# Decode's small copies made by ScalarE alone: placing the probabilities and spreading the queries in a hybrid decoder step

## The chip, the cores and the metric

The kernel runs on one core of one Trainium2 chip. The metric is the device time of one execution in microseconds (us), as a median over runs. The engines are TensorE (PE; its weight loads are PEld), VectorE (DVE), ScalarE (ACT), GpSimd (POOL) and SyncE (SP), which issues most DMAs. Each engine works through its own list of instructions in order and waits on semaphores for the others.

## What is computed

One layer of a hybrid decoder serves 512 prompt tokens and 32 sample tokens (8 sequences of 4) with shared weights, in float32. It is a feed-forward net, a mixer and a second feed-forward net, each with norms around it. The mixer has a gated linear recurrence (HGRN2) and latent softmax attention (MLA). The sample tokens also attend to 4096 past tokens each, whose latent rows (256 wide) and rotary keys (64 wide) lie in pages:

```python
def swiglu(x, wg, wu, wd):
    return (jax.nn.silu(x @ wg) * (x @ wu)) @ wd

# mla_attend, one block of queries
s = (jnp.einsum('bqhr,bsr->bhqs', ql, c_kv) + jnp.einsum('bqhd,bsd->bhqs', qr, k_rope)).astype(jnp.float32) * scale
s = jnp.where(k_pos[None, None, None, :] <= qp[None, None, :, None], s, -jnp.inf)
p = jax.nn.softmax(s, axis=-1).astype(c_kv.dtype)
return jnp.einsum('bhqs,bsr->bqhr', p, c_kv)

# layer
h = h + 0.5 * rmsnorm(swiglu(rmsnorm(h, norm_g[0]), wg[0], wu[0], wd[0]), norm_g[1])
m, c_kv, k_r, s_fin = mixer(rmsnorm(h, norm_g[2]), pos, past_ckv, past_kr, past_pos, s0, lb, ...)
h = h + rmsnorm(m, norm_g[3])
h = h + 0.5 * rmsnorm(swiglu(rmsnorm(h, norm_g[4]), wg[1], wu[1], wd[1]), norm_g[5])
```

## The kernel before

The tokens are split in two column parts, 0 and 1. The stages follow each other: the first feed-forward net, the mixer, then the second net for part 0 with the attention of the sample tokens to the past (decode) woven into it, then the output projection and the second net for part 1. Each product of two float32 matrices is made of three matmuls over a high and a low half of the operands. So each weight tile is loaded as `wraw`, ACT makes its high half `wh` by a cast (line 250), and DVE makes the low half `wl` as the difference (line 251). In the second net a gate product goes to DVE (`sil`, line 334), then through three ACT steps of a sigmoid (`sit`, lines 320 to 322), back to DVE (336), is multiplied by the up product (365) and split by ACT and DVE (170 and 171) into the operand of the down product (lines 259 and 288).

Decode handles each sample sequence in two halves of 2048 past tokens, 16 halves in all (class `Half`). A half goes through these steps:
- `gather`, `gather_r` (lines 1366, 1373): POOL issues indirect DMAs that bring latent rows and rotary keys into one of seven slots.
- `turn` (1381): DVE transposes pieces of these rows in 32 by 32 blocks into `kh`, ten for a half, two columns at a time.
- `score` (1393): PE multiplies the spread queries `qbd` by `kh` into two banks `s`; the results are copied to SBUF, one bank by ACT and one by DVE (1399), and DVE takes the row maximum (1401).
- `peak`: PE spreads the maximum (1405), DVE reduces it (1407) and makes the bias (1410), ACT takes the exponential (1411), DVE transposes it in blocks to `pt` (1413), and 16 copies place its blocks in `pbuf` (1417), in which each query's columns stand at its own place among zeros. Of each four copies, the one with g = 0 is made by DVE and the other three by ACT.
- `value` (1426): PE multiplies `pbuf` by the latent rows in two groups of eight products, c = 0 and c = 1; each reads the blocks of two of the four c of the copies. The sum is copied out by ACT (1429) and gathered by a small product (1434).

`qsplit` (1252) spreads the queries of one sequence: four copies out of `qrep`, which `decode_prep` has made (1243, 1245), into the operand `qbd` of the score products, each block at its own columns among zeros. Those of even g are made by DVE and those of odd g by ACT. It runs once for each of 8 sequences, and `qbd` has two buffers.

`decode()` is a generator that runs the steps of five halves at a time, each half some rounds behind the one before it; a round has five steps, `peak` is at its second step and `value` at its last. The loop at the end of the stage takes one step of decode and then as many steps of the net (`gb`) as keep the two in proportion (100 of the net's). This fixes the program's order. The order on each engine, and the slots of tiles, are then chosen by a planner with a timing model of its own, which follows the program's order as a priority; `tc.issue_after` adds an order by hand (the last `turn` of a round stands behind the maximum).

Of the kernel before, what the change touches and what calls it, by code (L numbers as in the profile page):

```python
# [110 lines left out]
def hybrid_step_kernel(  # L111
# [5 lines left out]
    nc = tc.nc  # L117
# [12 lines left out]
    def mk(shape, dt, tag, bufs=1, pool=None):  # L130
        return (pool or cur[-1]).tile(shape, dt, name=tag, tag=tag, bufs=bufs)
# [10 lines left out]
    def ps(name, tag="ps", own=False):  # L142
        if tag == "ps" and not own:
            tag = CYC[turns[0] % 4]
            turns[0] += 1
        return pp.tile([P, 512], F32, name=name, tag=tag, bufs=NPS[tag])
# [642 lines left out]
    with scope("mix") as mx_:  # L789
# [293 lines left out]
        with scope("at2"):  # L1083
# [163 lines left out]
            def qsplit(b):  # L1247
                q = qbd[b % 2]
                bs = slice(b * 16, b * 16 + 16)
                for g in range(4):  # L1250
                    gs = slice(g * 32, g * 32 + 32)
                    (nc.scalar.copy if g % 2 else nc.vector.tensor_copy)(q[gs, :, g % 2 * 16 : g % 2 * 16 + 16], qrep[gs, :, bs])

            def to_ffn(x):
                u4[x], part = parted_u(4, x)
# [7 lines left out]
            for i, (hd, x) in enumerate(heads):  # L1263
                if i + LOOK < len(heads):
                    if i + LOOK < NH:
                        prep(i + LOOK)
                    else:
                        qsplit_n(i + LOOK - NH, 1, qnb[:, i + LOOK - NH])
                    pe_.append(soft(*heads[i + LOOK]))
                if i < NH:  # L1270
                    latent(i)
                if i == PJ0:
                    pj = project(0, to_ffn)
                    next(pj)
                value(hd, x, pe_[i])
                if i == NH - 1:
                    dq = mk([P, 2, KQ * HS[1]], F32, "q1", pool=dK)
                    qbd = [dq[:, 0, k * 320 : (k + 1) * 320].rearrange("p (j q) -> p j q", j=10) for k in range(2)]
                    qrep = dq[:, 1, : 10 * P].rearrange("p (j q) -> p j q", j=10)
                    nc.gpsimd.memset(dq[:, 0, :640], 0.0)  # L1280
                if i == DP:
                    decode_prep()
                    qsplit(0)
                for _ in range(PJ[i]):
                    next(pj, None)
                if i in W1:
                    w0.append(weight([wcols((w_g, w_u)[W1.index(i)][1], 0, KD, 0)], KD))
# [14 lines left out]
    with scope("dec"):  # L1302
# [49 lines left out]
        class Half:  # L1352
# [31 lines left out]
            def score(self, st):  # L1384
                q = qbd[self.b % 2]
                if st == 0:
                    self.s = [ps("s", own=True) for _ in range(2)]
                for jj, j in enumerate(JS[st]):
                    for c in range(4):
                        for r in range(2):  # L1390
                            rs = slice(r * 64, r * 64 + 64)
                            kh = self.kh[st][rs, c // 2, c % 2 * 4 : c % 2 * 4 + 4, jj]
                            nc.tensor.matmul(self.s[r][c * 32 : c * 32 + 32, :P], q[rs, j], kh, start=st + jj == 0, stop=st == len(JS) - 1 and jj == 1, skip_group_check=True)  # L1393
                if st == 1 and self.i and self.b + 1 < NB:
                    qsplit(self.b + 1)
                if st < len(JS) - 1:
                    return
                for r in range(2):
                    (nc.vector.tensor_copy if r else nc.scalar.copy)(self.e[:, r * P : r * P + P], self.s[r][:, :P])
                self.mx = mk([P, 1], F32, "mxh", 2)  # L1400
                self.top = nc.vector.tensor_reduce(self.mx, self.e, axis=AX.X, op=ALU.max)

            def peak(self):
                pm = ps("pm", "pm")[:, :P]
                nc.tensor.matmul(pm, self.mx.broadcast_to([P, P]), ident, start=True, stop=True, skip_group_check=True)
                m = m3[:, self.i, self.bs]
                nc.vector.tensor_reduce(m, pm.rearrange("p (g q) -> p q g", q=16), axis=AX.X, op=ALU.max)
                mq = mk([P, 16], F32, "mq", 2)
                mb = mk([P, 1], F32, "mbd", 2)
                nc.vector.scalar_tensor_tensor(mq, m, -SCALE, selL, op0=ALU.mult, op1=ALU.mult, accum_out=mb)  # L1410
                nc.scalar.activation(self.e, self.e, AF.Exp, scale=SCALE, bias=mb, accum_out=Lc[:, self.i, 0, self.b : self.b + 1])
                pt = mk([P, ROWS, 32], F32, "pt", 2)
                nc.vector.transpose(pt.rearrange("p a k -> p (a k)"), self.e)  # L1413
                for c in range(4):
                    for g in range(4):
                        src = pt[c * 32 : c * 32 + 32, g // 2 * 4 : g // 2 * 4 + 4, g % 2 * 16 : g % 2 * 16 + 16]
                        (nc.scalar.copy if g else nc.vector.tensor_copy)(self.p[g * 32 : g * 32 + 32, c // 2, c % 2 * 4 : c % 2 * 4 + 4, self.i * 16 : self.i * 16 + 16], src)  # L1417

            def value(self, mate, c):
                i = self.i  # L1420
# [289 lines left out]
```

## Time and profile before

| | |
|---|---|
| median of 3 runs | 1250.35 us (1250.27 to 1250.57) |
| the profiled execution, own time | 1243.16 us |
| its span in the trace | 1241.4 us, granted clock 0.999 |
| decode's copies to `pbuf` (L1417) | 192 on ACT, 64 on DVE |
| spread of the queries (L1252) | 16 on ACT, 16 on DVE |

A profile is of one execution. Engines are listed with their busy time; "wl<-wraw,wh" is an instruction that writes the tile wl from wraw and wh, and L251 is a line of the kernel. Rows of a timeline give the start in us from the span's start, the length in us, the engine, line and operation, the shapes, how many were merged, and in brackets the engine's idle time before it and who ended it. The waits are listed as "who <- for whom: us in total, times, longest". The chain of waits goes back from the last instruction to what released it, or to the instruction before it on its engine. The decode stage is the stretch from 691 to 953 us.

### The profile page before, as it was taken

What the parts mean: (1) busy time and instruction counts of PE and PEld (TensorE: products, weight loads), DVE (VectorE), ACT (ScalarE), POOL (GpSimd) and SP (SyncE); (2) the same over time, 40 slices, a digit from 0 to 9 for tenths busy, and PEclk for the clock granted to TensorE, in tenths of its full rate; (3) what the DMA queues carried; (4) which work ended last, traced back from release to release, by engine and by line L of the source; (5) the groups of instructions that cost most, each with busy time, mean ns of one, the idle gap of its engine ahead of it and who ended that gap; (6) DMA issues with size and microseconds to landing.
All of it is one profiled execution on the core that took longest, in us unless ns stands there. A gap on an engine that the chain in (4) does not pass through costs nothing.

```text
span 1241.4 us, 29997 instructions
## 1 busy us (share of the span) xinstructions
PE 1215.0 (98%) x12366; PEld 1151.3 (93%) x12366; DVE 982.7 (79%) x1976; ACT 738.8 (60%) x1559; POOL 76.5 (6%) x80
## 2 busy tenths in 40 slices
PE   8999999999999999999999999999999999999997
PEld 6999999999999989988898888888888999999997
DVE  7897788878678888786877899999998778566665
ACT  7675545455366744545758766666656776554455
POOL 0000000000000000000001312322310000000000
PEclk9999999999999999999999999999999999999999
DMA  6232333232264213333233868878776635545451
GB/s 238 86 115 90 103 103 102 86 99 91 62 221 147 82 54 105 88 94 130 85 105 117 339 214 303 310 282 323 258 275 232 198 106 188 184 137 188 150 151 60
DMA packets 73113, 195.59 MB, mean 158 GB/s; under 512 B 12336, under 2 KB 27728, under 8 KB 68240
## 3 DMA queue, kind: packets, MB, share of 16 engines
q1 hardware_dynamic: 64512, 150.47, 37.3%
q0 software_dynamic: 7168, 41.95, 9.2%
q8 instruction: 97, 1.59, 0.5%
q10 hardware_dynamic: 1296, 1.26, 0.3%
q14 instruction: 40, 0.33, 0.1%
HBM read 183.97 MB, written 9.67 MB: 156 GB/s over the span
## 4 chain that ended last, share of the span: by engine, by line
PE 79%; DVE 11%; ACT 7%; issue 2%; DMA 2%; SPq 0%; DVEq 0%; ACTq 0%
PE acc L259 29%; PE acc L277 13%; PE dn L259 8%; PE Y L575 7%; PE X L575 4%; PE Z L575 4%; DVE kh L1381 3%; PE acc L731 3%; DVE wl L251 2%; ACT wh L250 1%; PE s L1393 1%; ACT pbuf L1417 1%; DMA wraw<-w_g 1%; PE pa L952 1%; PE o L1426 1%
## 5 line engine op out<-in xcount | busy, mean ns | idle before, releaser
L250 ACT CAST wh<-wraw 128x1024 fp32r<-128x1024 f32 (+2 forms) x194 | 185.0, 957 | 164.3 <-PE acc L259 103.7
L251 DVE TENSOR_TENSOR wl<-wraw,wh 128x1024 fp32r<-128x1024 f32 (+2 forms) x194 | 214.6, 1108 | 72.2 <-ACT wh L250 71.6
L277 PE MATMUL acc<-uha,wh 128*128 128x256 f32 (+1 forms) x528 | 155.5, 295 | 0.1
L277 PE MATMUL acc<-uha,wl 128*128 128x256 f32 (+1 forms) x528 | 150.0, 285 | 0.8 <-DVE wl L251 0.7
L277 PE MATMUL acc<-ula,wh 128*128 128x256 f32 (+1 forms) x528 | 150.5, 286 | 0.0
L259 PE MATMUL acc<-uhb,wh 128*128 128x288 f32 (+1 forms) x432 | 128.0, 296 | 0.0
L259 PE MATMUL acc<-uhb,wl 128*128 128x288 f32 (+1 forms) x432 | 127.0, 295 | 1.0 <-DVE wl L251 0.8
L259 PE MATMUL acc<-ulb,wh 128*128 128x288 f32 (+1 forms) x432 | 127.5, 295 | 0.0
L277 PEld LDWEIGHTS acc<-uha,wh 128*128 128x128 f32 x528 | 99.2, 188 | 8.8 <-issue 7.9
L277 PEld LDWEIGHTS acc<-uha,wl 128*128 128x128 f32 x528 | 99.2, 188 | 2.3 <-DVE wl L251 1.6
L277 PEld LDWEIGHTS acc<-ula,wh 128*128 128x128 f32 x528 | 99.4, 188 | 1.6 <-issue 1.2
L259 PEld LDWEIGHTS acc<-uhb,wl 128*128 128x128 f32 x432 | 81.2, 188 | 1.6 <-DVE wl L251 1.6
L259 PEld LDWEIGHTS acc<-uhb,wh 128*128 128x128 f32 x432 | 81.0, 187 | 0.2 <-ACT uhb L170 0.2
L259 PEld LDWEIGHTS acc<-ulb,wh 128*128 128x128 f32 x432 | 81.1, 188 | 0.1
L259 PE MATMUL dn<-hh,dh 128*128 128x272 f32 x256 | 74.3, 290 | 0.0
L259 PE MATMUL dn<-hh,dl 128*128 128x272 f32 x256 | 73.7, 288 | 0.0
L259 PE MATMUL dn<-hl,dh 128*128 128x272 f32 x256 | 73.6, 288 | 0.0
L277 PE MATMUL acc<-uhb,wh 128*128 128x272 f32 x176 | 52.8, 300 | 0.0
L1417 ACT COPY pbuf<-pt 32x64 f32<-32x64 f32 x192 | 46.5, 242 | 10.1 <-DVE pt L1413 7.3
L259 PE MATMUL acc<-hlb,wh 128*128 128x288 f32 x176 | 52.1, 298 | 0.0
L259 PE MATMUL acc<-hhb,wh 128*128 128x288 f32 x176 | 51.8, 298 | 0.0
L1393 PE MATMUL s<-kh,q 64*32 64x128 f32 x2560 | 48.0, 273 | 3.5 <-DVE kh L1381 3.5
(632 smaller groups left out, 3881.3 us busy)
## 6 DMA issues: line engine op xcount, KB each, us to landing
wraw<-w_u SPq DMA_DIRECT2D x66, 512.0 KB, 4.3
wraw<-w_g SPq DMA_DIRECT2D x65, 512.0 KB, 3.9
wraw<-w_d SPq DMA_DIRECT2D x40, 384.0 KB, 3.5
wraw<-w_in SPq DMA_DIRECT2D x24, 512.0 KB, 3.5
wraw<-w_d SPq DMA_DIRECT2D x32, 320.0 KB, 3.1
wraw<-w_d SPq DMA_DIRECT2D x16, 512.0 KB, 3.8
wraw<-w_o SPq DMA_DIRECT2D x16, 512.0 KB, 3.7
g_S<-state SPq DMA_DIRECT2D x4, 512.0 KB, 4.4
```

The source lines that it names most:

```text
L250: nc.scalar.copy(wh[:, :kt], w[:, :kt])
L251: nc.vector.tensor_tensor(wl[:, :kt], w[:, :kt], f32(wh[:, :kt]), op=ALU.subtract)
L259: nc.tensor.matmul(out, a, b, start=n == 0, stop=n == last)
L277: nc.tensor.matmul(acc[:, :n], a[:, k], b[:, k], start=k + i == 0, stop=k == kt - 1 and i == 2)
L575: nc.tensor.matmul(bank, a[p][:, k], b[q][:, k], start=first and k + n == 0, stop=k == 3 and n == 2, skip_group_check=True)
L731: nc.tensor.matmul(accs[x, d], wts[d][p][:, k], hs[k // 2][q][:, k % 2, x], start=k + n == 0, stop=k == nf - 1 and n == 2)
L952: nc.tensor.matmul(po[es, c].rearrange("p (n m) -> p n m", m=m), kx[:, cs], up(qx[:, cs], m), start=True, stop=True, skip_group_check=True)
L1381: nc.vector.transpose(kh[:, g].rearrange("p a j k -> p a (j k)"), src)
L1393: nc.tensor.matmul(self.s[r][c * 32 : c * 32 + 32, :P], q[rs, j], kh, start=st + jj == 0, stop=st == len(JS) - 1 and jj == 1, skip_group_c ...
L1417: (nc.scalar.copy if g else nc.vector.tensor_copy)(self.p[g * 32 : g * 32 + 32, c // 2, c % 2 * 4 : c % 2 * 4 + 4, self.i * 16 : self.i * ...
L1426: nc.tensor.matmul(o[g : g + 32, :R], self.p[:, c, a], self.craw[c][:, a], start=i + c == 0 and a < 4, stop=i + c == 2 and a >= 4, skip_gr ...
```

## The change

All 16 copies of `peak` and all 4 copies of `qsplit` are made by ScalarE. Per half, 4 of the 16 copies of 32 x 64 elements go from DVE to ACT, 64 in all; per sequence, 2 of the 4 copies of 32 x 160 elements, 16 in all. The copies read and write what they did before, and their place in the program's order stays. No other line differs.

```diff
             def qsplit(b):
...
-                    (nc.scalar.copy if g % 2 else nc.vector.tensor_copy)(q[gs, :, g % 2 * 16 : g % 2 * 16 + 16], qrep[gs, :, bs])
+                    nc.scalar.copy(q[gs, :, g % 2 * 16 : g % 2 * 16 + 16], qrep[gs, :, bs])
...
             def peak(self):
...
-                        (nc.scalar.copy if g else nc.vector.tensor_copy)(self.p[g * 32 : g * 32 + 32, c // 2, c % 2 * 4 : c % 2 * 4 + 4, self.i * 16 : self.i * 16 + 16], src)
+                        nc.scalar.copy(self.p[g * 32 : g * 32 + 32, c // 2, c % 2 * 4 : c % 2 * 4 + 4, self.i * 16 : self.i * 16 + 16], src)
```

## The prediction

> **What bounds the kernel now.** I read the page's engine shares first, then the busy time of each engine by stretches of the decode stage, then what waits for what there, then the chain of waits, and last the order of instructions on ScalarE (ACT) and VectorE (DVE) around the copies that move.
>
> ```profile
> PE 1215.0 (98%) x12366; PEld 1151.3 (93%) x12366; DVE 982.7 (79%) x1976; ACT 738.8 (60%) x1559; POOL 76.5 (6%) x80
> ```
>
> Over the whole span TensorE (PE) is the full engine. All copies that move start between 666 and 951 us, so only that stage counts. Cut where its regimes change (columns: stretch, its length, then busy us and instructions of PE, PEld, DVE, ACT, POOL, the clock, DMA):
>
> ```profile
> 753.00:797.60 44.60, 44.43 (x806) 39.48 (x806) 40.45 (x85) 28.95 (x78) 13.28 (x12) 1.00 0.89 317
> 797.60:839.00 41.40, 39.98 (x818) 34.30 (x818) 39.27 (x90) 26.82 (x76) 12.81 (x12) 1.00 0.77 270
> 884.40:943.00 58.60, 58.16 (x1105) 50.25 (x1103) 54.41 (x122) 34.74 (x95) 11.91 (x11) 1.00 0.70 243
> sum 262.00, PE 255.78 PEld 224.28 DVE 244.06 ACT 166.56 POOL 65.31; mean PE 42.63 PEld 37.38 DVE 40.68 ACT 27.76 POOL 10.89
> ```
>
> The sum runs from 691 to 953 us. PE idles 262.00 - 255.78 = 6.2 us in it: no help to any other engine can gain more than about that. DVE is nearly as full (39.27 of 41.40), ACT is not (26.82). In 753 to 797.6 PE is the bound; in 797.6 to 839 it idles 1.4 us, and there the question is whether DVE or ACT is late.
>
> ```profile
> DVE wl L251 <- ACT wh L250: 16.8, 21, 2.9
> PEld s L1393 <- DVE kh L1381: 5.4, 7, 1.7
> PE s L1393 <- DVE kh L1381: 3.5, 7, 1.4
> PEld o L1426 <- ACT pbuf L1417: 1.9, 5, 0.6
> ```
>
> DVE, though full, itself waits 16.8 us for ACT's casts (wh); PE waits for DVE's transposes (kh), and in five places for ACT's pbuf copies. So the two engines hand a chain to and fro. The chain of waits says how much of it is the copies:
>
> ```profile
> by line: DVE kh L1381 25.9%; ACT pbuf L1417 12.5%; DVE wl L251 11.6%; issue 7.4%; ACT wh L250 6.8%; PE s L1393 4.2%; ACT sit L321 3.6%; DVE hla L171 3.1%; DVE sil L336 3.0%; ACT sit L322 3.0%; DVE sil L365 2.5%; ACT sit L320 2.2%; DVE mxh L
> 808.84 0.24 ACT pbuf L1417
> ...
> 950.65 0.24 ACT pbuf L1417
> ...
> 735.86 0.14 DVE pbuf L1417
> ...
> 937.44 0.04 DVE pbuf L1417
> ...
> 742.71 0.15 DVE q L1252
> ...
> 891.55 0.24 DVE q L1252
> ```
>
> The first line is of 797 to 840 us. Below it stand the first and the last piece of each kind: 72 pieces of ACT's pbuf copies, which are all 12 of a half in 6 of the 16 halves; 16 pieces of DVE's, in 4 halves; 8 pieces of DVE's spread of the queries, 1.4 us together. The copies that lie on the chain are ACT's more than DVE's. That decides my forecast: the change lengthens the link that is late more often.
>
> **The change part by part.** Prices first (minimum/median/maximum ns):
>
> ```profile
> L1417 ACT COPY pbuf<-pt x192: 239/242/247, 735.5 to 950.6; 32x64 f32<-32x64 f32 x192
> L1417 DVE COPY pbuf<-pt x64: 140/183/188, 735.9 to 948.4; 32x64 f32<-32x64 f32 x64
> L1252 DVE COPY q<-q x16: 223/234/257, 666.1 to 891.6; 32x160 f32<-32x160 f32 x16
> L1252 ACT COPY q<-q x16: 320/324/327, 666.8 to 887.3; 32x160 f32<-32x160 f32 x16
> ```
>
> [...]
>
> In a row the copies run at this pace, and this stands around them (times of start, length):
>
> ```profile
> 808.84 3.07 ACT L1417 COPY pbuf<-pt 32x64 f32<-32x64 f32 x12 [1.16 <-DVE pt L1413]
> 811.93 1.05 ACT L250 CAST wh<-wraw 128x1024 fp32r<-128x1024 f32 x1
> 813.86 0.42 ACT L322 ACTIVATE sit<-sit 128x256 f32<-128x256 f32 x1
> ...
> 809.32 0.74 DVE L1417 COPY pbuf<-pt 32x64 f32<-32x64 f32 x4
> 813.00 1.23 DVE L251 TENSOR_TENSOR wl<-wraw,wh 128x1024 fp32r<-128x1024 f32 x1 [0.73 <-ACT wh L250]
> 814.31 0.43 DVE L336 TENSOR_TENSOR sil<-sil,sit 128x256 f32<-128x256 f32 x1
> ```
>
> A half's 12 copies take 3.07 us on ACT, 0.256 each; 16 will take 4.1, that is 1.02 more. DVE loses its four, 0.75 us. Behind the copies on ACT stand the cast of the next weight (wh, 0.02 us after the last copy) and the three steps of the gate's sigmoid (sit); DVE waits for the cast already (0.73 us idle) and then for sit. Freeing DVE's 0.75 us here only makes that idle time longer: the next link moves by the full 1.02 us.
>
> So I cost the old chain anew with the order of instructions kept. It is a lower bound of the stage's new length, since the links stay dependent and another path can only be longer.
> - Probabilities on ACT: 6 halves by 4 copies by 0.256 = +6.1 us.
> - Probabilities on DVE: 4 halves by 0.75 = -3.0 us.
> - Spread on DVE: -1.4 us.
> - Spread on ACT: two spreads run together at 666 us, six later ones alone. The later ones lie ahead of an idle time of ACT, shortest at 742 and next at 828, against 0.67 us for two copies more:
>
> ```profile
> 743.05 0.84 ACT L250 CAST wh<-wraw 128x768 fp32r<-128x768 f32 x1 [0.29 <-PE acc L277]
> ...
> 747.61 0.92 DVE L251 TENSOR_TENSOR wl<-wraw,wh 128x768 fp32r<-128x768 f32 x1
> ...
> 827.69 0.67 ACT L1252 COPY q<-q 32x160 f32<-32x160 f32 x2
> 829.13 0.84 ACT L250 CAST wh<-wraw 128x768 fp32r<-128x768 f32 x1 [0.77 <-PE acc L277]
> ...
> 666.83 1.00 ACT L1252 COPY q<-q 32x160 f32<-32x160 f32 x3
> 667.85 1.05 ACT L250 CAST wh<-wraw 128x1024 fp32r<-128x1024 f32 x1
> ```
>
> At 742 only 0.29 of 0.67 is covered by ACT's wait, but DVE's share of that weight comes 3.7 us after the cast, behind transposes, so it hides the rest; I take nothing for the six. If their cover were gone they would cost 6 by 0.67 = 4.0 us. The two at 666.83 have a cast right behind three of their copies: three more by 0.333, +1.0 us.
>
> Together +6.1 - 3.0 - 1.4 + 1.0 = +2.7 us.
>
> What is late next: the value matmuls, which read pbuf. In the two halves where DVE's copies hold up kh and PE stalls most, ACT's own copies end just ahead of value's second group:
>
> ```profile
> 836.79 3.06 ACT L1417 COPY pbuf<-pt 32x64 f32<-32x64 f32 x12 [0.66 <-DVE pt L1413]
> ...
> 838.54 0.42 PE L1393 MATMUL s<-kh,q 64*32 64x128 f32 x8 [1.11 <-DVE kh L1381]
> 839.71 1.07 PE L1426 MATMUL o<-ulb,pbuf 128*32 128x256 f32 x16
> 840.59 1.05 PE L1426 MATMUL o<-uhb,pbuf 128*32 128x256 f32 x16
> ```
>
> The copies end at 839.85 and the second group starts at 840.59: 0.74 us of room for 1.02 more. PE's stall on kh gets 0.75 us shorter, and the second group then waits until 0.28 us past its old start. So the relief is taken back and more: 1.03 us in each of the two halves, at 836.79 and, with the same layout, near 751: +2.1 us. The sum is +2.7 + 2.1 = **+4.8 us**.
>
> The cost of a move of PE's value group is bounded: POOL's gathers and the copy of the sum (os) wait for it, but the next half's value lies some 13 us later. Weights come on SP's queue, which nothing here is moved past; SP waits for free raw tiles, which a cast 1 us late frees 1 us late. In the stretch from 753 to 797.6, PE reaches value 3 to 4 us after the copies end (they lie beside PE work), so those halves cost nothing.
>
> The profiled execution took 1243.16 us (span 1241.4), 7.2 us under the median of the timed runs. The sum is a difference within that execution, 1243.2 + 4.8 = 1248.0, and I add it to the median: 1250.35 + 4.8 = **1255.2 us**.
>
> **The rivals.**
> *DVE's relief wins (faster).* DVE loses 64 by 0.19 and 16 by 0.25, 16 us, of the engine that is 93% busy in the stage (244.06 of 262.00), and ACT at 64% takes 22 us in its idle time. The rule in the Trainium skill's page Perfetto Trace Analysis, section Identifying the Most-Contended Engine, says the same: help the engine with the highest occupancy. For it speak PE's waits for kh (3.5 us); the most it could give is the 6.2 us idle. It decides if the casts are issued ahead of the copies on ACT, so that a copy delays only value, and value's room of 0.4 to 0.8 us grows with DVE's lead. Then about the 3.5 us are won: 1246.8. Against it is the row with wh 0.02 us behind the copies.
>
> *PE covers it (no change).* PE is 98% busy, and 6.2 us of idle in 262 leave little to shift; stalls early in a gate phase shorten the later stall for kh instead of adding to it. Then +6.1 on ACT and the 4.4 of DVE's relief meet in stalls that exist anyway: 1250.4, at most 2 us to either side.
>
> *The order is replanned (slower yet).* The program's order on each engine comes from a planner; with ACT fuller it may put the copies behind a cast or a sigmoid, or spread sets ahead of one. If one cast (1.05 us) comes ahead of the copies in 5 halves where value has under 1 us of room, value waits 5 us more: 1259.8.
>
> **How the numbers follow.** Forecast 0.52, DVE's relief 0.15, no change 0.20, replanned 0.13. About 0.2%, 2.5 us, is what a measurement of this kernel can tell from no change. Slower takes the replanned case and most of the forecast (its lower bound, +2.7, lies at the border): 0.61. Within 0.2%: 0.25. Faster: 0.14. The range goes from the relief's 3.4 us of gain, 1247.0, to just short of the replanned case, 1259.0; the forecast's own range is 1252.8 to 1258.0.
>
> **What would show it.** In the changed profile: L1417 with 256 copies on ACT at 242 ns and none on DVE; a half's copies 4.1 us in a row, with wh right behind; DVE's waits for ACT wh up from 16.8 us by some 5; PEld o's waits for pbuf up from 1.9 us to 5 or more; PE's waits for kh down from 3.5 but not to none; ACT pbuf on the chain in at least 6 halves; the decode stage (691 to 953) some 4 us longer and the rest unchanged. I am wrong if the waits for pbuf do not grow, if casts stand ahead of the copies, or if the time is lost outside this stage.

## The result, and the profile after

The changed kernel takes 1256.03 us, median of 6 runs (1254.18 to 1258.16); the kernel before, on the same chip, 1250.31 (1249.65 to 1251.63). The ratio is 1.0045, 95% interval 1.0035 to 1.0055: slower by 5.7 us (4.4 to 6.9). Forecast were +4.8 us and slower. The profiled execution of the changed kernel took 1256.2 us.

The execution of before that the prediction was read from took 1243.2 us, and the timed ones 1250. So the unaltered kernel was profiled once more (e0 below, 1251.7 us); from here on the profiles of the changed kernel stand beside that one where the two profiles of before differ.

The page of the changed kernel, the engine shares and the chain that ended last:

```profile
PE 1224.0 (98%) x12366; PEld 1155.7 (92%) x12366; DVE 968.0 (77%) x1896; ACT 757.9 (60%) x1639; POOL 69.7 (6%) x80
...
PE 88%; DVE 5%; ACT 4%; DMA 2%; issue 1%; DVEq 0%; SPq 0%; ACTq 0%
```

ACT is 19 us fuller and DVE 15 us emptier than before, about as priced. But the chain runs through PE for 88% of the span (86% in e0, 79% in the first profile). Of the changed kernel's waits from 680 to 965 us, those that bear on this, in the order of their totals:

```profile
DVE wl L251 <- ACT wh L250: 27.6, 21, 2.5
PEld s L1393 <- issue: 13.2, 25, 0.8
PE s L1393 <- issue: 6.3, 19, 0.6
PEld o L1426 <- ACT pbuf L1417: 2.6, 4, 0.9
PE o L1426 <- ACT pbuf L1417: 0.9, 3, 0.4
```

And the same of the kernel before in its second profile, e0:

```profile
DVE wl L251 <- ACT wh L250: 16.1, 20, 2.9
PEld s L1393 <- issue: 6.6, 12, 0.8
PE s L1393 <- issue: 3.3, 11, 0.6
PEld s L1393 <- DVE kh L1381: 2.9, 4, 1.4
PE s L1393 <- DVE kh L1381: 1.8, 4, 1.1
PEld o L1426 <- ACT pbuf L1417: 1.7, 4, 0.6
```

DVE waits 11.5 us more for ACT's casts: the relief has become idle time. The waits for kh are all but gone (0.2 us). The waits for pbuf have hardly grown. What has doubled is "issue" ahead of the score matmuls (line 1393): PE and its weight loads stand still there, and the profile names nobody they wait for. One half shows how. The changed kernel's timeline (other rows left out):

```profile
798.27 4.08 ACT L1417 COPY pbuf<-pt 32x64 f32<-32x64 f32 x16 [0.84 <-DVE pt L1413]
...
799.69 1.26 DVE L1381 STREAM_TRANSPOSE kh<-rraw 128x512 f32<-128x512 f32 x2
800.15 1.46 PE L1393 MATMUL s<-kh,q 64*32 64x128 f32 x49
800.62 0.95 POOL L1373 DMA_INDIRECT rraw<-pool_r,idx  x1 [8.36 <-DVE kh L1381]
801.88 0.95 POOL L1373 DMA_INDIRECT rraw<-pool_r,idx  x1 [0.30 <-issue]
801.93 0.42 PE L1393 MATMUL s<-kh,q 64*32 64x128 f32 x3 [0.32 <-issue]
802.38 1.05 ACT L250 CAST wh<-wraw 128x1024 fp32r<-128x1024 f32 x1
802.63 0.43 PE L1393 MATMUL s<-kh,q 64*32 64x128 f32 x5 [0.29 <-issue]
803.37 0.44 PE L1393 MATMUL s<-kh,q 64*32 64x128 f32 x7 [0.30 <-issue]
...
803.74 1.07 PE L1426 MATMUL o<-uhb,pbuf 128*32 128x256 f32 x16
```

The same half of the kernel before (e0):

```profile
800.26 3.06 ACT L1417 COPY pbuf<-pt 32x64 f32<-32x64 f32 x12 [0.85 <-DVE pt L1413]
...
802.14 1.16 PE L1393 MATMUL s<-kh,q 64*32 64x128 f32 x64
802.48 1.26 DVE L1381 STREAM_TRANSPOSE kh<-rraw 128x512 f32<-128x512 f32 x2
803.23 1.07 PE L1426 MATMUL o<-uhb,pbuf 128*32 128x256 f32 x16
...
803.42 0.95 POOL L1373 DMA_INDIRECT rraw<-pool_r,idx  x1 [9.17 <-DVE kh L1381]
```

Before, the half's second run of 64 score matmuls goes through in one piece of 1.16 us, and GpSimd (POOL) issues the next gather of rotary keys after it, at 803.42. In the changed kernel DVE, rid of its four copies, begins the transposes of rraw 0.46 us ahead of the score run and not 0.34 us behind its start; POOL, which waits for them ("<-DVE kh"), issues at 800.62, inside the score run. The run now comes in pieces of 49, 3, 5 and 7, and value starts at 803.74, 3.6 us after the run's start instead of 1.1. The 16 copies had ended at 802.35 and held up no matmul of value. I call these breaks pauses. The chain of waits of the changed kernel in the stretch of 797 to 840 us is PE's own work with pauses in it:

```profile
by line: PE acc L277 55.8%; PE s L1393 23.4%; PE o L1426 13.0%; issue 5.5%; PE pm L1405 1.5%; PE o L1434 0.9%
...
801.21 0.39 PE s L1393 x3
801.60 0.32 issue
801.93 0.42 PE s L1393 x3
```

This table counts, from the start of one score matmul to the start of the next, the steps of 0.50 to 0.65 us (in a whole run a step is some 0.014), and adds up the 32 runs of score matmuls of the stage from first start to last start, with the waits for kh that fall inside them:

| kernel | pauses | 32 score runs, us | time against before of the same batch |
|---|---|---|---|
| before, first profile | 2 | 41.3 | |
| before, e0 | 9 | 46.1 | |
| e2, spread alone | 10 | 46.8 | 0.0 us |
| e3, DVE's copies left out | 15 | 50.5 | +4.6 |
| changed | 17 | 51.8 | +5.7 |
| changed again, e11 | 17 | 52.3 | +5.0 |
| e1, probabilities alone | 19 | 53.8 | +7.8 |
| e4, before, later gathers | 0 | 44.1 | -3.0 |
| e5, changed, later gathers | 1 | 41.8 | +2.2 |

From e0 to the changed kernel the runs grow by 5.7 us, what the kernel lost. In the rows from e0 to e1 the time follows this column. The last two rows show that this is not all.

Not every step of that length is a pause: the profile gives both of the first profile's, and two of e0's (at 814.94 and 902.56 us), to waits for kh. So the first profile has none and e0 has seven. The pauses go with the gathers, but a gather beside a score run isn't enough. From the second half on there are 30 score runs. In the changed kernel 12 of them have a rotary gather issued beside them; all 17 pauses lie in ten of these, and the other 18 runs have none. In the first profile six have one, and none of the six breaks; here is one of them:

```profile
854.38 0.95 POOL L1373 DMA_INDIRECT rraw<-pool_r,idx  x1 [0.31 <-DVE wl L251]
854.81 1.16 PE L1393 MATMUL s<-kh,q 64*32 64x128 f32 x64
```

Nor do six such runs of e10 below, on the chip that runs the kernel before in 1243.9 us. The first profile's execution took 1243.2 us; its chip isn't on record.

### The profile page after: what moved, and what is told of

Its sections match the earlier page's. It is cut to its first block, busy times and chain, and to the rows that moved or that the text cites. A ratio compares the mean times of both kernels' runs of the same rounds, so it can differ in the third digit from the quotient of the medians.

```text
span 1254.4 us, 29998 instructions
## 1 busy us (share of the span) xinstructions
PE 1224.0 (98%) x12366; PEld 1155.7 (92%) x12366; DVE 968.0 (77%) x1896; ACT 757.9 (60%) x1639; POOL 69.7 (6%) x80
## 4 chain that ended last, share of the span: by engine, by line
PE 88%; DVE 5%; ACT 4%; DMA 2%; issue 1%; DVEq 0%; SPq 0%; ACTq 0%
PE acc L259 30%; PE acc L277 17%; PE dn L259 8%; PE Y L575 6%; PE X L575 4%; PE Z L575 4%; PE s L1393 4%; PE acc L731 3%; PE o L1426 2%; PE pa L952 1%; PE acc L288 1%; ACT wh L250 1%; PE s L1202 1%; DVE wl L251 1%; DMA wraw<-w_g 1%
## 5 line engine op out<-in xcount | busy, mean ns | idle before, releaser
L1417 ACT COPY pbuf<-pt 32x64 f32<-32x64 f32 x256 | 62.0, 242 | 9.3 <-DVE pt L1413 6.0
L1393 PE MATMUL s<-kh,q 64*32 64x128 f32 x2560 | 55.2, 273 | 6.8 <-issue 6.3
L1393 PEld LDWEIGHTS s<-kh,q 64*32 64x32 f32 x2560 | 39.2, 105 | 18.2 <-issue 13.2
```

What stands on the lines that cost most here:

```text
L1417: nc.scalar.copy(self.p[g * 32 : g * 32 + 32, c // 2, c % 2 * 4 : c % 2 * 4 + 4, self.i * 16 : self.i * 16 + 16], src)
```

## The experiments

Two theories stood against each other. The chain theory is the prediction's: ACT's longer row of copies makes value late. The pause theory: DVE's relief lets POOL issue earlier, and the gathers cut the score runs. Kernels of one batch ran on one chip, and only those are compared: before took 1249.82 us (e0 to e3), 1250.60 (e4 to e7), 1243.89 (e8 to e10) and 1250.91 (e11).

**e0, the kernel before again.** No edit.

> The kernel before, unchanged, for a second profile of it. The profiled execution of before that the prediction reads took 1243.2 us, its timed runs 1250.3; the changed kernel's profiled one took 1256.2 like its timed ones. If the chain theory holds alone (ACT's longer row of copies delays the cast and the value matmuls), this profile has TensorE running through each half's second run of score matmuls (64 matmuls in about 0.9 us) as in the first profile. If the changed profile's other feature, pauses of 0.57 us within those runs with nothing that the profile names, belongs to the chip and the day and not to the change, this profile shows them too, some 12 of them or 7 us, and a span near 1249.

1251.73 us, one run; its lines stand above. In this execution the granted clock was 0.82 from 691 to 720 us (0.94 in the changed kernel's), which is at most 29 x 0.18 = 5.2 us of its length; every score run but the first begins after that stretch. The unaltered kernel has pauses of its own, seven here, which the first profile didn't show.

**e1, the probabilities alone.** Only line 1417 of the change.

```diff
-                        (nc.scalar.copy if g else nc.vector.tensor_copy)(self.p[...], src)
+                        nc.scalar.copy(self.p[...], src)
```

> Only the probabilities' copies go to ScalarE; the spread of the queries stays as before. Chain theory: +6.1 on ACT's copies, -3.0 on DVE's, +2.1 taken back at value: +5.2 us, 1255.5; at least +3. Rival, that it is the spread that costs (its cover on ACT gone): within 1 us of before. Rival, that any shift of order does it: no relation to the sum, for instance as much as the whole change or nothing.

1257.65 us, ratio 1.0058 (1.0045 to 1.0071): all of the loss comes from this part (its interval and the whole change's, 1.0035 to 1.0055, overlap).

**e2, the spread alone.** Only line 1252.

```diff
-                    (nc.scalar.copy if g % 2 else nc.vector.tensor_copy)(q[...], qrep[gs, :, bs])
+                    nc.scalar.copy(q[...], qrep[gs, :, bs])
```

> Only the spread of the queries goes to ScalarE; the probabilities' copies stay split. Chain theory: -1.4 on DVE, +1.0 on ACT at the first two spreads: -0.4 us, that is no change within 1.5 us. Rival, that the spread's cover is gone: +4 us or more.

1249.78 us, ratio 1.0000 (0.9991 to 1.0009): it costs nothing and brings nothing.

**e3, DVE's relief without ACT's extra copies.** The copies of g = 0 are left out.

```diff
             def peak(self):
...
-                    for g in range(4):
+                    for g in range(1, 4):
```

> VectorE's four copies of each half are left out and nobody makes them (the rows of g = 0 of the placed probabilities stay zero, so a quarter of the heads' products is left out); the spread stays split. This is DVE's relief by itself, without ACT's price. Chain theory: DVE's 0.75 us was on the chain in 4 halves: -3.0 us at most, and the relief is taken back in part by value's wait for ACT's other copies, so -1 to -3 us, 1247.3 to 1249.3. The rival in which DVE is the bound of the stage: -3.5 us or more, up to the 6 us that TensorE idles. If nothing is gained, DVE's copies were hidden, and the change could only lose.

1254.46 us, ratio 1.0037 (1.0023 to 1.0051). Less work, and 4.6 us slower. Its waits from 680 to 965 us:

```profile
PEld s L1393 <- issue: 12.5, 24, 1.2
PEld o L1426 <- ACT pbuf L1417: 1.7, 4, 0.6
```

The waits for pbuf are those of before (1.7), and the pauses are nearly those of the change (12.5 of 13.2). The chain theory can't give a loss here: ACT's row is the old one. It had forecast -1 to -3 us.

**e4 and e5, the rotary gathers later.** In e4 the kernel before, in e5 the changed kernel; the next half's rotary gathers are queued on POOL behind the latent gathers, which wait for value.

```diff
-                nc.gpsimd.indirect_dma_start(craw..., None, pool_c, off)
+                Half.last = nc.gpsimd.indirect_dma_start(craw..., None, pool_c, off)
...
-                    if st == 0 and h_.n + 1 < NH2:
-                        H[h_.n + 1].gather_r()
+                    if st == 1 and h_.n + 1 < NH2:
+                        with tc.issue_after(Half.last.ins):
+                            H[h_.n + 1].gather_r()
```

> The kernel before, with the gathers of the rotary keys (rraw) queued on GpSimd behind the latent gathers that wait for the value matmuls; so they are no longer issued beside the second run of score matmuls. Pause theory: TensorE stops for 0.57 us at a time in that run while a rotary gather is being issued; the second profile of before has about 6.6 us of such pauses, so they go and the time falls by 4 to 6 us, 1244 to 1246. Chain theory (ACT's copies delay the cast and value): the gathers do not matter, within 1 us of 1249.8, or slower if the keys then come late for VectorE's transposes.

> The changed kernel with the same later rotary gathers. Pause theory: its 13 us of pauses go, so it falls by 9 to 13 us, to 1243 to 1247, and lies within 2 us of the kernel before with later gathers: then the change's cost was the meeting of the gathers with the score run. Chain theory: it stays some 5 us above the kernel before with later gathers.

e4: 1247.60 us, ratio 0.9981 (0.9972 to 0.9990), the one kernel of this batch that beats both. e5: 1252.84 us, ratio 1.0019 (1.0010 to 1.0028). The pause theory's 1244 to 1246 for e4 was missed by 1.6 us; its 1243 to 1247 for e5, within 2 us of e4, was missed altogether. Of the waits of e4, then of e5, 680 to 965 us:

```profile
PEld s L1393 <- DVE kh L1381: 6.0, 11, 1.2
PE s L1393 <- DVE kh L1381: 3.4, 6, 1.1
PEld o L1426 <- ACT pbuf L1417: 2.7, 8, 0.6
PEld s L1393 <- issue: 1.8, 5, 0.5
```

```profile
PEld o L1426 <- ACT pbuf L1417: 16.2, 26, 0.9
PE o L1426 <- ACT pbuf L1417: 5.4, 16, 0.4
PEld s L1393 <- DVE kh L1381: 3.8, 8, 1.0
PEld s L1393 <- issue: 2.1, 3, 1.1
```

With the gathers moved, the pauses are gone from both kernels but for one in e5. The move has a price of its own: in e4 PEld waits 6.0 us for kh (2.9 in e0), and the rotary gathers' transfers are 7.1% of the chain from 691 to 960 us. And now the prediction's wait is there: PEld waits 16.2 us for pbuf in e5 against 2.7 in e4, and ACT's pbuf copies are 16.0% of that chain against 7.1%. The same half as above, in e5's timeline:

```profile
797.92 4.08 ACT L1417 COPY pbuf<-pt 32x64 f32<-32x64 f32 x16 [0.93 <-DVE pt L1413]
...
800.03 1.07 PE L1426 MATMUL o<-uhb,pbuf 128*32 128x256 f32 x16
...
802.06 0.64 PE L1426 MATMUL o<-ha,pbuf 128*32 128x256 f32 x8 [0.38 <-ACT pbuf L1417]
```

The last eight value matmuls (the trace holds two for each product) start at 802.06, right behind the copies' end at 802.00: value's second group waits, as forecast. From e4 to e5 the change costs 1252.84 - 1247.60 = +5.2 us with a single pause in it.

**e6, rotary keys of the first half only; e7, rotary keys by SyncE.** Both on the changed kernel. In e6 the later halves read the first half's keys; in e7 SyncE loads as many bytes from rows that the list of indices doesn't choose.

```diff
             def gather_r(self):
...
+                if self.n:
+                    self.rraw = Half.kept
+                    return
+                Half.kept = self.rraw
```

```diff
-                    nc.gpsimd.indirect_dma_start(rraw..., None, pool_r, off)
+                    nc.sync.dma_start(rraw..., pool_r[blk * P : blk * P + P])
```

> The changed kernel in which the rotary keys are gathered for the first half alone and used for all 16 (the other halves' rotary part of the scores is left out, replaced by that of the first). No rotary gather is issued in the stage. Pause theory: no pauses of 0.57 us in the second score run, time 1243 to 1247. If the pauses stay, they belong to the score matmuls or to ACT's copies and not to GpSimd's gathers. Chain theory: within 2 us of the changed kernel, 1256.

> The changed kernel with the rotary keys loaded by plain DMAs of SyncE's queue, the same bytes from other rows (the paging of the rotary keys is left out). It parts GpSimd's issue from the transfer: if the pauses come from GpSimd's writing of the gather, none are left; if they come from the rotary rows landing, they stay, at other places. The time itself is no test, since SyncE then waits for free rotary tiles ahead of weights.

e6: 1250.38 us, ratio 0.9997 (0.9988 to 1.0006). e7: 1252.01 us, one run. Of the waits of the score's weight loads for "issue" two are left in e6 and one in e7 (2.8 and 1.1 us in all), and both have the wait for pbuf, which the pause theory's 1243 to 1247 us for e6 had left out. Here it is in e7's waits of 680 to 965 us (line 1425 is before's 1426):

```profile
PEld o L1425 <- ACT pbuf L1416: 13.4, 24, 0.9
PE o L1425 <- ACT pbuf L1416: 4.3, 13, 0.4
```

In e7 SyncE issues rotary keys inside six of the runs of 64, or at most 1.4 us ahead of them; they land 2.7 to 4.6 us after the issue, and none of the six breaks. So the pauses go with POOL's gather, not with as many bytes from SyncE. In both kernels the order of other instructions changes too, so their times say less than their waits.

**e8, e9, e10: the kernel before with later gathers and another share of the copies.** e8 leaves DVE's copies out as e3 does, e9 gives DVE those of g = 0 and 1 (8 and 8), e10 gives those of g = 0 to POOL. The edit of e4, and:

```diff
-                        (nc.scalar.copy if g else nc.vector.tensor_copy)(self.p[...], src)
+                        (nc.scalar.copy if g > 1 else nc.vector.tensor_copy)(self.p[...], src)
```

```diff
-                        (nc.scalar.copy if g else nc.vector.tensor_copy)(self.p[...], src)
+                        (nc.scalar.copy if g else nc.gpsimd.tensor_copy)(self.p[...], src)
```

> The kernel before with later rotary gathers, and VectorE's four copies of each half left out (rows of g = 0 of the placed probabilities stay zero, so a quarter of the heads' products is left out). With the pauses gone this is VectorE's relief alone. My forecast's working: -3 us less what value takes back, so 1245 to 1247.6 against 1247.6. If relief itself is harmful without any pause, above 1249. Where it is nothing, VectorE's copies are hidden, and the 5.2 us between the two kernels with later gathers are all ACT's price.

> The kernel before with later rotary gathers and one more copy of each four on VectorE: 8 of a half on each engine. If value's wait for ACT's row is what costs in the changed kernel, it shrinks here by 1.02 us a half: PEld o's wait for pbuf goes from 2.7 us to about none, and VectorE's extra 0.75 us a half lands on TensorE's waits for kh: 1246 to 1250. If ACT's row were the stage's bound, below 1246; if VectorE is, above 1250.

> The kernel before with later rotary gathers and the copies of g = 0 made by GpSimd: VectorE is relieved and ACT's row stays at 12. If GpSimd's four copies end before ACT's twelve (3.07 us), the time is that of the kernel that leaves them out, 1245 to 1247.6; if they are slower than 0.77 us each, value waits for them and the time rises above 1249.

e8: 1246.37 us, ratio 1.0017 (1.0008 to 1.0026). e9: 1254.38, ratio 1.0092 (1.0076 to 1.0109), above 1250, which was expected if DVE became the bound. e10: 1252.51, ratio 1.0089 (1.0064 to 1.0114). The chip of this batch ran the kernel before in 1243.89 us, and e4 wasn't run on it; so what the later gathers themselves cost there isn't known, and e8's +2.5 us doesn't tell whether relief without pauses brings something. The other two, with the same gathers, lie 8.0 and 6.1 us above e8. Of the waits of e9 and of e10, 680 to 965 us:

```profile
PEld s L1393 <- DVE kh L1381: 15.4, 14, 3.1
PE s L1393 <- DVE kh L1381: 11.6, 12, 2.8
```

```profile
PEld o L1426 <- POOL pbuf L1417: 10.0, 8, 3.8
PE o L1426 <- POOL pbuf L1417: 6.1, 5, 3.3
```

Four copies more on DVE make PE wait 11.6 us for kh; four on POOL make value wait for POOL, up to 3.3 us at a time. That isn't the length of a copy, which on POOL is 227 ns at the median against 242 on ACT: POOL's copies stand behind rotary gathers of its own and wait for these to land.

```profile
POOL pbuf L1417 <- DMA rraw<-pool_r,idx: 42.8, 12, 6.1
```

So 8 and 8, and a share for POOL, lose to the kernel before; 12 and 4 with later gathers wasn't run on this chip.

**e11, the changed kernel again.** No edit, in another batch.

> The changed kernel once more, unaltered, beside the kernel before. Pause theory (GpSimd's earlier rotary gathers cut the score runs): if the kernel before takes about 1250 us here, the changed one takes 5 to 6 us more, with 12 us or more of PEld's idle time in front of the score matmuls that the profile gives to no one (issue), and under 1 us of PE's waits for pbuf. If the kernel before takes about 1244 us here (a chip on which its own score runs are not cut), two cases: the pauses come with the chip, then they are missing here too, PEld's waits for pbuf are 13 us or more as in the changed kernel with later gathers, and the time is 1244 + 5 = 1249 us; or the earlier gathers make them on any chip, then issue is again 12 us or more and the time is 1250 to 1256 us. Chain theory (ScalarE's longer row alone): 1249 us there with waits for pbuf, and no dependence on the chip.

1255.95 us, ratio 1.0039 (1.0027 to 1.0051), before 1250.91. Of its waits:

```profile
PEld s L1393 <- issue: 13.7, 25, 1.1
PEld o L1426 <- ACT pbuf L1417: 2.6, 4, 0.9
```

The pauses stand in the same halves, 17 of them again; this is no accident of one execution. The chip was one of those with 1250 us, so whether the change brings pauses on the chip with 1243.9 us wasn't seen.

## Why the prediction was right or wrong

Sign, size (+5.7 against +4.8) and stage were right: from the second half's first score run to the start of the last run the changed kernel takes 216.1 us (734.51 to 950.60) and e0 210.9 (736.17 to 947.04), which is 5.2 us less. The mechanism, ACT's longer row, is real but is not the one at work in the kernel as changed, where DVE's relief does the harm. That +4.8 came so near is in good part luck.

- **Prices: right.** The row of the changed kernel (its last figure counts one form of two):

```profile
L1417 ACT COPY pbuf<-pt x256: 227/242/247, 736.0 to 963.9; 32x64 f32<-32x64 f32 x128
```

256 copies at 242 ns, a half's row 4.08 us (forecast 4.1), the cast 0.03 us behind it (802.38). The order wasn't replanned: the copies stand ahead of the casts.

- **DVE waits for ACT: right in sign, 11.5 us and not some 5.** DVE gets no nearer to its work; it waits.

- **The relief as a gain, -3.0 and -1.4 us: the step that failed.** I counted that DVE's share leaves the chain and that PE's stall on kh gets shorter, and of POOL I looked only at the gathers that wait for value. In the changed kernel the stall on kh does go, all but altogether; but POOL's rotary gathers wait for DVE's transposes, and in the same waits it says so:

```profile
POOL rraw L1373 <- DVE kh L1381: 125.0, 16, 13.5
```

An earlier DVE is an earlier POOL, and its gathers fall on the score run. e3 has the relief alone and loses 4.6 us where my steps give a gain of 3.0. The profile I read couldn't warn of it: in that execution a gather beside a score run cost nothing. The rule of the Trainium skill's page Perfetto Trace Analysis (Identifying the Most-Contended Engine), to optimize the engine with the highest occupancy first, doesn't agree with e3 when DVE, 93% busy in the stage, is taken for that engine: with less work on it the kernel takes 4.6 us more.

- **The probabilities on ACT, +6.1, and value's second group, +2.1: hidden in the changed kernel, shown without the pauses.** I was to be wrong if the waits for pbuf did not grow. They grew by 0.9 us on PEld (1.7 to 2.6), not to the 5 I asked for, and the chain from 691 to 960 us holds a single piece of ACT's pbuf copies where I wanted six halves. The score run, made longer by the pauses, ends after the copies do, so value has nothing left to wait for. In e5, where the pauses are gone but for one, the wait is 16.2 us, the waits for kh are down but not to none (3.8 us of 6.0 in e4), and the cost is +5.2, near the +4.8 of the sum.

- **The spread, +1.0 at 666 us: not there.** In the changed kernel three copies start at 666.50 and the cast follows at 667.55; before it came at 667.85. Taking nothing for the others was right (e2: 1.0000).

- **The rivals.** Relief that wins needed casts ahead of copies, and e3 speaks against it. That PE covers it is out by the interval.

So two stalls lie at the same place, just ahead of value, and cover each other: the relief with its pauses costs 4.6 us (e3), the change with all but one of the pauses taken away 5.2 (e5 against e4), and the change as it stands 5.7. They don't add, and the 5.7 can't be split between them. As the kernel runs, the pauses are the later of the two.

Left open is why a score run pauses: the traces of the chips that take 1250 us show that it mostly does so when POOL issues rotary gathers beside it (ten of twelve runs in the changed kernel), and that it doesn't when they come later or from SyncE. Why such gathers do nothing in the first profile and in e10, and what PE waits for in these 0.57 us, they don't name. So what the change costs on a chip without pauses isn't known.

## What to carry to other kernels

Relief of a full engine is not free: follow what it releases, through every queue that waits for it, to what runs at that moment. When two stalls end at the same place, the later hides the other, so a mechanism is shown only once the other has been taken away; a time that fits doesn't show it. And profile the kernel before more than once, when the profiled execution's own time lies off the median.

## What the runs showed of the hardware

- A dense run of small TensorE matmuls (64 of them, 1.16 us) can break off for some 0.57 us from one start to the next, up to three times, when GpSimd issues indirect gathers beside it: 17 times in the changed kernel, 0 and 1 times with the gathers later. It need not: in the first profile six such runs with a gather beside them go through whole, as do six runs of 96 in e10.
- The kernel before takes 1243.9 us on one chip and 1249.8 to 1250.9 on others. How much of that is pauses isn't known: the first profile (1243.2 us) has none, the second (1251.7 us) seven.
